# A hybrid encoder block on one core: folds of the long convolutions made two jobs ahead, inverse results handled behind the next job's products, inverse tables loaded with the forward ones

## The chip, the core and the metric

The kernel runs on one core of a Trainium2 chip. Five engines work from queues of their own, each in the order of its program: TensorE (PE) multiplies matrices into the eight banks of PSUM, VectorE (DVE), ScalarE (ACT) and GpSimd (POOL) do elementwise work, SyncE (SP) issues most DMAs. ScalarE and GpSimd issue some DMAs too, from the same queues as their arithmetic. An instruction that waits holds up all that stand behind it on its engine. The metric is the device time of one execution in microseconds, as the median of several.

## What is computed

One layer of an encoder block over 512 tokens of width 1024: a norm, a wide projection, a gated linear recurrence (branch A), a long convolution branch (branch B), a merge, and a mixture of 16 experts. The change touches branch B alone:

```python
hy = dwconv(hy, conv_b_w[l], conv_b_b[l], ...)        # width-3 convolution along the sequence
v, x1, x2 = jnp.split(hy, HYENA_ORDER + 1, axis=-1)   # each (1, 512, 1024)
z = v
for n, gate in enumerate((x1, x2)):
    k = bidir_kernel(filt[:, n, 0], filt[:, n, 1])    # length 1024
    z = gate * fftconv(z, k, filt_bias[l, n])         # irfft(rfft(z) * rfft(k)) + z * bias
y_b = z @ w_b_out[l]
```

So there are two long convolutions in a row (n = 0, 1), each over 1024 channels, and each followed by a gate.

## The kernel before

**Order.** The scheduler is told to keep the order in which the program emits instructions (`tc.manual_schedule()`, L106). A helper, `Defer` (L71 to L93), holds closures back: `df.at(lag, fn, prio)` queues one, `df.tick()` advances a counter and emits all that are due, by time, then by `prio`, then by age. So the place of a step in each engine's queue is set by the tick at which it falls due.

**The long convolutions as matmuls.** Channels are taken in eight blocks of 128; a job (n, j) is two blocks, i = 2j and 2j + 1, of convolution n. There are eight jobs, (0,0) to (0,3) and then (1,0) to (1,3); the text calls them jobs 0 to 7. Each value is split in a high part (rounded to the matmul's format by ScalarE) and a low part (what is left, by VectorE or GpSimd), and each product is three matmuls. The steps of a job:

- *fold* (`fold`, L490): sums and differences of the two halves of `z`, 128 by 512, mirrored; the sum on VectorE, the difference on GpSimd, into a tile `eo`. Two per job.
- *transposes* (`eo_trans`, L496): four per block on TensorE into one PSUM tile, the high part `eoh` by ScalarE, the low part `eol` by VectorE.
- *forward* (`fwd`, L526): 48 matmuls with the tables FC and FS (high and low parts) into four PSUM tiles. Then the products with the filter's spectrum (`K`, loaded from DRAM by `k_load`, L517), per tile: one multiplication on VectorE (`pr`), two additions on GpSimd (`y`), the high part on ScalarE (`yh`), the low part on VectorE (`yl`).
- *inverse* (`inv`, L569): per block 24 matmuls of `yh` and `yl` with the tables IC and IS.
- *result* (`inv_post`, L585): a copy on ScalarE (`qs`), two additions and a multiply-add on VectorE (`yt`), the gate's multiplication on GpSimd (`z`). For n = 0 this `z` is what job (1, j) folds; for n = 1 it is stored to DRAM (`z2d`) by a DMA that ScalarE issues (i < 6) or GpSimd (i = 6, 7).

**The loop** (L761 to L773). Per job: folds of the next job; forward and products of this one; loads of the next K; two projections (`x_slot`, 24 matmuls each, from the list `fill`), which give the gates x1 and x2 of later jobs and whose width-3 convolution (`conv3`: ScalarE, then two multiply-adds on VectorE) falls due one tick later; two inverses. The transposes of the next job fall due at the tick of the first projection (lag 2 in `job_prep`), the result of each inverse one tick after it: the first at the second inverse's tick, the second at the next forward's tick, ahead of the products.

**Weights of the projections** (`ahead`, L247). A projection's weights are loaded by SyncE into a ring (`wring`), split by ScalarE (high) and GpSimd (low) into `whl`, two projections ahead. `ahead` runs in each `slot()` (every projection) and in `fwd_slot`. The next high part waits until the projection that used its buffer has ended.

**Ahead of the loop** (L708 to L717). After the filter stage the tables FC and FS are loaded from GpSimd's queue, the first K from SyncE's, job 0 is folded, and two projections run, with the split of FC and FS between them. IC and IS are loaded from SyncE's queue behind the products of job 0 and split by ScalarE and GpSimd.

**Behind the loop** one projection runs (L931), then the gates of the recurrence (`lru_gates`, L828), whose operands VectorE casts (`wg_prep`, `parts_of`). The expert weights are loaded much later, from L1080 on.

**Buffers.** PSUM has eight banks in one pool (`ps_`, L148); a new tile takes the bank whose last reader stands first in the order of the program.

Of the kernel before, what the change touches and what calls it, by code (L numbers as in the profile page):

```python
# [12 lines left out]
F32R = mybir.dt.float32r  # L13
# [21 lines left out]
for _n, _w in (("g_mix", 8), ("ca_w", 32), ("ca_b", 8), ("b_r", 16), ("b_i", 16), ("lam", 16),  # L35
# [13 lines left out]
    "zz": ("left", dict(z=9, gx=6)),  # L49
# [4 lines left out]
    "H": ("left", dict(eo=2, pr=2, eoh=2, eol=2, FCh=1, FCl=1, FSh=1, FSl=1, K=4, y=2, yh=5, yl=5, ICh=1, ICl=1,  # L54
# [47 lines left out]
def block_kernel(ctx, tc, A, out, dbg=None):  # L102
# [34 lines left out]
    def f(ap):  # L137
        return ap.bitcast(F32)
# [251 lines left out]
    def table_load(nm, q):  # L390
        r = t_([128, 2, 512], nm="pr").rearrange("p a b -> p (a b)")
        q.dma_start(out=r, in_=A[nm])
        return r

    def table(nm, shape, r=None):
        r = table_load(nm, SY) if r is None else r
        r = r.rearrange("p (a b) -> p a b", a=shape[1])
        h = t_(shape, F32R, nm=nm + "h")
        l = t_(shape, F32R, nm=nm + "l")
        act(h, r)  # L400
        tt(G, l, r, f(h), ALU.subtract)
        return h, l
# [106 lines left out]
    def job_prep(n, j):  # L509

        for i in (2 * j, 2 * j + 1):
            eo = fold(zt[n, i])
            df.at(2, lambda i=i, eo=eo: eo_trans(n, i, eo))
# [173 lines left out]
    for q, (n, hf) in enumerate(jobs):  # L687
# [13 lines left out]
        if q < 3:  # L701
            parts = filt_prep(*wfb[q + 1])
            fill.pop(0)() if q < 2 else df.tick()
        else:
            df.tick()
        filt_b(n, hf, 1, im)
# [3 lines left out]
    tabs = [table_load(nm, G) for nm in ("FC", "FS")]  # L710
    k_load(0, 0)
    job_prep(0, 0)
    fill.pop(0)()
    FC = table("FC", [128, 2, 512], tabs[0])
    FS = table("FS", [128, 2, 512], tabs[1])
    fill.pop(0)()
    assert not fill  # L717

    def inv_slot(n, i):
        df.tick()  # L720
        p = inv(n, i)
        df.at(1, lambda: inv_post(n, i, p))

    def fwd_slot(n, j):
        ahead()
        df.tick()
        fwd(n, j)
# [33 lines left out]
    for q, (n, j) in enumerate(cjobs):  # L761
        if q + 1 < 8:
            job_prep(*cjobs[q + 1])
        fwd_slot(n, j)
        if q == 0:
            IC = table("IC", [128, 4, 256])
            IS = table("IS", [128, 4, 256])
        if q + 1 < 8:
            k_load(*cjobs[q + 1])
        for _ in range(2):  # L770
            fill.pop(0)()
        inv_slot(n, 2 * j)
        inv_slot(n, 2 * j + 1)  # L773
# [772 lines left out]
```

## Time and profile before

| | us |
|---|---|
| median of 3 runs | 1643.46 (1640.3 to 1644.1) |
| the profiled execution | 1639.69 |
| its span, from the first to the last instruction | 1637.9 |
| TensorE busy | 1545.1 (94%) |
| VectorE busy | 592.6 (36%) |
| GpSimd busy | 374.0 (23%) |
| ScalarE busy | 371.2 (23%) |
| mean granted clock of TensorE | 0.977 |

The shares are means over stages that differ. Up to about 690 us TensorE has what it needs in SBUF and the DMAs move 85 to 230 GB/s; from there on the expert weights stream in at some 427 GB/s. The long convolutions lie between 136 and 352 us. The profile's views give, for each engine, busy time in a stretch, the single instructions with the idle time ahead of them and what ended it, and the spread of one instruction's length.

### The profile page before, as it was taken

How to read it: one execution, taken by the hardware profiler on the slowest of the kernel's cores; microseconds unless marked ns; L12 is line 12 of the kernel's file. 1: busy time of each engine (PE TensorE's matmuls, PEld its weight loads, DVE VectorE, ACT ScalarE, POOL GpSimd, SP SyncE). 2: the span in 40 equal slices, each digit the busy share in tenths (PEclk: the TensorE clock that was granted, in tenths of full speed). 3: DMA queues.
4: the chain of work that ended last, by engine and by line, in shares of the span. 5: the costliest groups of instructions: out<-in, count | busy, mean ns of one | idle time of the engine just before them, and what ended most of it. 6: DMA issues, size and time to landing. Idle time of an engine off the chain costs nothing.

```text
span 1637.9 us, 17943 instructions
## 1 busy us (share of the span) xinstructions
PE 1545.1 (94%) x7364; PEld 895.4 (55%) x7364; DVE 592.6 (36%) x878; ACT 371.2 (23%) x576; POOL 374.0 (23%) x257
## 2 busy tenths in 40 slices
PE   7999899999999999899999999999999999989997
PEld 5788888888888888733443343343343343333332
DVE  7887778776676644321001101101002002011102
ACT  5543323337655633301010000100100100100011
POOL 3647565655567742000000000000000000000000
PEclk9999999999999999999999999999999999999999
DMA  6566523443433336879999999999999999999996
GB/s 200 155 202 210 154 85 109 142 142 92 114 90 92 90 101 224 351 297 387 407 426 427 426 428 426 428 426 427 427 427 428 426 426 428 427 427 427 426 425 269
DMA packets 140813, 492.26 MB, mean 301 GB/s; under 512 B 8674, under 2 KB 103202, under 8 KB 115644
## 3 DMA queue, kind: packets, MB, share of 16 engines
q1 hardware_dynamic: 138048, 487.34, 75.7%
q0 software_dynamic: 592, 2.07, 0.4%
q10 hardware_dynamic: 2092, 1.72, 0.3%
q8 instruction: 58, 0.95, 0.2%
q14 instruction: 23, 0.19, 0.0%
HBM read 473.82 MB, written 17.30 MB: 300 GB/s over the span
## 4 chain that ended last, share of the span: by engine, by line
PE 49%; DMA 12%; DVE 2%; issue 1%; ACT 1%; POOLq 0%; ACTq 0%; DVEq 0%; SPq 0%
PE q L1261 23%; PE q L1296 11%; DMA we<-in_w_up_dram 6%; PE q L1311 4%; PE ps L244 3%; PE ps L1117 3%; PE q L1227 2%; DMA hz<-in_w_up_dram 2%; DMA whl<-in_w_down_dram 2%; DMA hz<-in_w_down_dram 2%; PE q L1283 1%; PE q L1354 1%; DMA out_dram<-hh 0%; DVE pm L1177 0%; PE q L1246 0%
## 5 line engine op out<-in xcount | busy, mean ns | idle before, releaser
L1261 PE MATMUL q<-we,xe 128*64 128x512 f32 x1088 | 340.6, 597 | 17.8 <-DMA we<-in_w_up_dram 8.1
L244 PE MATMUL ps<-hT,whl 128*128 128x512 f32 x1320 | 307.5, 392 | 0.6 <-POOL whl L132 0.6
L244 PEld LDWEIGHTS ps<-hT,whl 128*128 128x128 f32 x1320 | 248.4, 189 | 53.8 <-POOL whl L132 1.1
L132 POOL TENSOR_TENSOR whl<-wring,whl 128x1024 fp32r<-128x1024 f32 x72 | 181.0, 2517 | 146.2 <-ACT whl L129 66.7
L1465 POOL DMA_INDIRECT out_dram<-we,idx x1 | 1.1, 1097 | 925.5 <-DVE we L135 925.5
L1261 PEld LDWEIGHTS q<-we,xe 128*64 128x64 f32 x1088 | 103.8, 137 | 190.9 <-issue 172.6
L1296 PE MATMUL q<-we,sgy 128*64 128x512 f32 x576 | 183.2, 621 | 4.2 <-ACT sgy L129 3.6
L132 DVE TENSOR_TENSOR xe<-q,cv 128x512 f32<-128x512 f32 (+1 forms) x22 | 11.5, 543 | 468.8 <-PE q L1261 427.0
L1261 PE MATMUL q<-hz,xe 128*64 128x512 f32 x480 | 160.3, 603 | 3.6 <-DMA hz<-in_w_up_dram 2.7
L129 ACT ACTIVATE sgy<-q 128x512 f32<-128x512 f32 x80 | 45.2, 596 | 394.9 <-PE q L1283 221.5
L132 DVE TENSOR_TENSOR xm<-xm,q 128x512 f32<-128x512 f32 x56 | 38.5, 687 | 208.1 <-PE q L1311 208.1
L1261 PE MATMUL q<-wring,xe 128*64 128x512 f32 x240 | 109.4, 604 | 0.8 <-DVE xe L132 0.8
L129 ACT ACTIVATE pm<-q 128x512 f32<-128x512 f32 x7 | 4.2, 597 | 454.4 <-PE q L1246 403.1
L1296 PEld LDWEIGHTS q<-we,sgy 128*64 128x64 f32 x576 | 54.1, 142 | 84.2 <-issue 76.1
L129 ACT ACTIVATE whl<-wring 128x1024 fp32r<-128x1024 f32 x72 | 76.2, 1058 | 91.1 <-PE ps L244 46.8
L1261 PE MATMUL q<-whl,xe 128*64 128x512 f32 x208 | 93.3, 596 | 3.4 <-issue 2.0
L244 PE MATMUL ps<-hA,whl 128*128 128x512 f32 x384 | 89.2, 391 | 0.0
L1261 PEld LDWEIGHTS q<-hz,xe 128*64 128x64 f32 x480 | 48.2, 138 | 62.6 <-issue 55.9
L244 PEld LDWEIGHTS ps<-hA,whl 128*128 128x128 f32 x384 | 72.1, 188 | 15.8
L1296 PE MATMUL q<-hz,sgy 128*64 128x512 f32 x224 | 75.2, 612 | 1.5 <-ACT sgy L129 1.5
L1311 PE MATMUL q<-sgy,pm 128*128 128x512 f32 x112 | 62.7, 642 | 0.0
L1296 PE MATMUL q<-whl,sgy 128*64 128x512 f32 x128 | 61.2, 623 | 1.5 <-DMA whl<-in_w_down_dram 1.5
(316 smaller groups left out, 2071.2 us busy)
## 6 DMA issues: line engine op xcount, KB each, us to landing
we<-in_w_down_dram SPq DMA_DIRECT2D x36, 2048.0 KB, 30.9
we<-in_w_up_dram SPq DMA_DIRECT2D x35, 2048.0 KB, 29.1
we<-in_w_gate_dram SPq DMA_DIRECT2D x33, 2048.0 KB, 29.1
wring<-in_w_in_dram SPq DMA_DIRECT2D x56, 512.0 KB, 4.8
hz<-in_w_gate_dram SPq DMA_DIRECT2D x14, 2048.0 KB, 27.8
hz<-in_w_down_dram SPq DMA_DIRECT2D x12, 2048.0 KB, 31.3
hz<-in_w_up_dram SPq DMA_DIRECT2D x12, 2048.0 KB, 28.3
whl<-in_w_gate_dram SPq DMA_DIRECT2D x8, 2048.0 KB, 30.7
```

The costliest lines, as they stand in the source:

```text
L129: P.activation(out=out, in_=in_, func=func, **kw)
L132: e.tensor_tensor(out=out, in0=a, in1=b, op=op)
L244: T.matmul(p, lhsT=a[:, k, :], rhs=b[k], start=(n == 0), stop=(n == 23))
L1117: T.matmul(p, lhsT=a[k][:, i * 128:(i + 1) * 128], rhs=wo[q][b][:, k, :], start=(n == 0), stop=(n == 23))
L1227: T.matmul(p[:, k * 128:(k + 1) * 128], lhsT=src[:, i, u * 128 * R + r:(u + 1) * 128 * R:R], rhs=pm[:, i, :], start=(i == 0), stop=(i == 3))
L1261: T.matmul(out[q][o:o + 64], lhsT=xe[:, k, o:o + 64], rhs=w[:, r * 2048 + q * 512:r * 2048 + (q + 1) * 512], start=(k == 0), stop=(k == KT ...
L1283: T.transpose(p[:, j * 128:(j + 1) * 128], sg[:, u * 128 * RD + i:(u + 1) * 128 * RD:RD], ident)
L1296: T.matmul(acc[hf][o:o + 64], lhsT=st[:, j % 4 * 128 + o:j % 4 * 128 + o + 64], rhs=w[:, i * 1024 + hf * 512:i * 1024 + (hf + 1) * 512], s ...
L1311: T.matmul(p, lhsT=sc[:, i * 128:(i + 1) * 128], rhs=ye[:, hf * 512:(hf + 1) * 512], start=True, stop=True)
L1354: T.matmul(p, lhsT=pm[:, i, :], rhs=xm[:, i, hf * 512:(hf + 1) * 512], start=(i == 0), stop=(i == 3))
L1465: G.indirect_dma_start(out=out, out_offset=bass.IndirectOffsetOnAxis(ap=last["idx"], axis=0), in_=yo, in_offset=None, bounds_check=S - 1, ...
```

## The change

Four things are moved.

- **Folds.** `job_prep` is split in `job_fold` and `job_turn`. Job q + 2 is folded between the two inverses of job q (job 0 in the filter stage, job 1 between the splits of FC and FS). The transposes of job q + 1 fall due at the tick of job q's second projection, so they come between the two projections and no longer ahead of both. The pool of `eo` is opened earlier for that.
- **Results.** The results of both inverses fall due at the tick of the next job's first projection (lags 3 and 2, with priority 0), behind the next products. For job 7 the lags stay 1.
- **Tables.** IC goes into a tile of its own (`raw`), IS in two halves into the two `xa` tiles, all issued from GpSimd's queue with FC and FS, and their low parts are made by VectorE ahead of job 0.
- **Weights.** `ahead` moves from `fwd_slot` to `inv_slot`.

```diff
@@ -46,12 +46,12 @@
     "W": ("right", dict(wring=1, whl=1)),
     "A": ("right", dict(hT2=1)),
     "bx": ("right", dict(xa=2)),
-    "zz": ("left", dict(z=9, gx=6)),
+    "zz": ("left", dict(z=9, gx=6, eo=2)),
     "S": ("left", dict(Sh=1, Sl=1, S0=1)),
     "F0": ("right", dict(x=4, junk=1, zT=1, w2=1, sa=1, sk=1, s=2)),
     "F": ("left", dict(dec=4, wf=1, wb=1, wc=2, wst=4, ed=4, KCh=1, KCl=1, KSh=1, KSl=1, pr=1, EDh=8, EDl=8, bs=2,
                        kr=3, ki=4)),
-    "H": ("left", dict(eo=2, pr=2, eoh=2, eol=2, FCh=1, FCl=1, FSh=1, FSl=1, K=4, y=2, yh=5, yl=5, ICh=1, ICl=1,
+    "H": ("left", dict(pr=2, raw=1, eoh=2, eol=2, FCh=1, FCl=1, FSh=1, FSl=1, K=4, y=2, yh=5, yl=5, ICh=1, ICl=1,
                        ISh=1, ISl=1, qs=1, yt=2)),
     "mB": ("left", dict(mB=8, hF=8, tg=3)),
     "hA": ("left", dict(hA=8)),
@@ -387,18 +387,18 @@
         return out
 
 
-    def table_load(nm, q):
-        r = t_([128, 2, 512], nm="pr").rearrange("p a b -> p (a b)")
+    def table_load(nm, q, tag="pr"):
+        r = t_([128, 2, 512], nm=tag).rearrange("p a b -> p (a b)")
         q.dma_start(out=r, in_=A[nm])
         return r
 
-    def table(nm, shape, r=None):
+    def table(nm, shape, r=None, e=G):
         r = table_load(nm, SY) if r is None else r
         r = r.rearrange("p (a b) -> p a b", a=shape[1])
         h = t_(shape, F32R, nm=nm + "h")
         l = t_(shape, F32R, nm=nm + "l")
         act(h, r)
-        tt(G, l, r, f(h), ALU.subtract)
+        tt(e, l, r, f(h), ALU.subtract)
         return h, l
 
 
@@ -506,11 +506,15 @@
         act(hi[:, :, c0:c0 + 128], pv)
         tt(V, lo[:, :, c0:c0 + 128], pv, f(hi)[:, :, c0:c0 + 128], ALU.subtract)
 
-    def job_prep(n, j):
-
-        for i in (2 * j, 2 * j + 1):
-            eo = fold(zt[n, i])
-            df.at(2, lambda i=i, eo=eo: eo_trans(n, i, eo))
+    eos = {}
+
+    def job_fold(n, j):
+
+        eos[n, j] = [fold(zt[n, 2 * j + e]) for e in range(2)]
+
+    def job_turn(n, j):
+        for e, eo in enumerate(eos.pop((n, j))):
+            eo_trans(n, 2 * j + e, eo)
 
     Ks, Y = {}, {}
 
@@ -703,26 +707,38 @@
             fill.pop(0)() if q < 2 else df.tick()
         else:
             df.tick()
+            job_fold(0, 0)
         filt_b(n, hf, 1, im)
         df.tick()
     close_("F", "S")
     open_("H", "bx")
     tabs = [table_load(nm, G) for nm in ("FC", "FS")]
+    tabs.append(table_load("IC", G, "raw"))
+    half = [t_([128, 512], nm="xa") for _ in range(2)]
+    for a in range(2):
+        G.dma_start(out=half[a], in_=A["IS"][:, a * 512:(a + 1) * 512])
     k_load(0, 0)
-    job_prep(0, 0)
     fill.pop(0)()
     FC = table("FC", [128, 2, 512], tabs[0])
+    job_turn(0, 0)
     FS = table("FS", [128, 2, 512], tabs[1])
+    job_fold(0, 1)
     fill.pop(0)()
     assert not fill
-
-    def inv_slot(n, i):
+    IC = table("IC", [128, 4, 256], tabs[2], V)
+    IS = [t_([128, 4, 256], F32R, nm=nm) for nm in ("ISh", "ISl")]
+    for a in range(2):
+        h, l = (v[:, 2 * a:2 * a + 2].rearrange("p a b -> p (a b)") for v in IS)
+        act(h, half[a])
+        tt(V, l, half[a], f(h), ALU.subtract)
+
+    def inv_slot(n, i, lag):
+        ahead()
         df.tick()
         p = inv(n, i)
-        df.at(1, lambda: inv_post(n, i, p))
+        df.at(lag, lambda: inv_post(n, i, p), 0)
 
     def fwd_slot(n, j):
-        ahead()
         df.tick()
         fwd(n, j)
 
@@ -759,18 +775,18 @@
         return proj(hTh, hTl)
 
     for q, (n, j) in enumerate(cjobs):
-        if q + 1 < 8:
-            job_prep(*cjobs[q + 1])
         fwd_slot(n, j)
-        if q == 0:
-            IC = table("IC", [128, 4, 256])
-            IS = table("IS", [128, 4, 256])
         if q + 1 < 8:
             k_load(*cjobs[q + 1])
-        for _ in range(2):
-            fill.pop(0)()
-        inv_slot(n, 2 * j)
-        inv_slot(n, 2 * j + 1)
+        fill.pop(0)()
+        if q + 1 < 8:
+            df.at(1, lambda v=cjobs[q + 1]: job_turn(*v))
+        fill.pop(0)()
+
+        inv_slot(n, 2 * j, 3 if q < 7 else 1)
+        if q + 2 < 8:
+            job_fold(*cjobs[q + 2])
+        inv_slot(n, 2 * j + 1, 2 if q < 7 else 1)
 
     for _ in rates:
         pass
```

## Rows read from the trace of the kernel before

**Rows 1.** Windows of four jobs: window, length, busy PE PEld DVE ACT POOL, PEclk, DMA share

```profile
150.21:176.04 25.83, 23.80 (x154) 21.49 (x153) 17.94 (x26) 10.97 (x15) 15.49 (x12) 1.00 0.63 185
...
227.65:254.07 26.42, 24.09 (x155) 21.43 (x153) 21.67 (x34) 7.39 (x12) 15.36 (x14) 1.00 0.34 100
...
305.73:329.04 23.31, 23.31 (x154) 21.39 (x153) 18.74 (x24) 7.50 (x12) 15.00 (x14) 1.00 0.49 139
...
329.04:352.10 23.06, 22.69 (x147) 20.59 (x145) 16.46 (x21) 5.86 (x9) 13.43 (x13) 1.00 0.24 77
```

**Rows 2.** Timeline of PE, 141 to 170 and 305 to 330: start, length, what, idle before

```profile
141.93 0.60 PE L503 MATMUL ps<-ident,eo 128*128 128x128 f32 x4
...
144.28 0.63 PE L503 MATMUL ps<-ident,eo 128*128 128x128 f32 x4 [1.75 <-DVE eo L132]
...
144.66 5.72 PE L244 MATMUL ps<-hT,whl 128*128 128x512 f32 x24
...
311.49 1.03 PE L503 MATMUL ps<-ident,eo 128*128 128x128 f32 x8
...
312.28 11.18 PE L244 MATMUL ps<-hT,whl 128*128 128x512 f32 x48
...
323.29 0.64 PE L578 MATMUL ps<-ICh,yh 128*128 128x256 f32 x4
```

**Rows 3.** Waits, 136 to 350 us: engine, line, awaited, total, times, longest

```profile
PE ps L503 <- POOL eo L132: 5.2, 5, 1.5
...
PE ps L578 <- ACT yh L129: 4.5, 6, 1.0
```

**Rows 4.** Timeline of DVE and ACT, products of jobs 0 and 6

```profile
155.16 2.34 DVE L132 TENSOR_TENSOR pr<-ps,K 128x1024 f32<-128x1024 f32 x2
...
313.12 2.34 DVE L132 TENSOR_TENSOR pr<-ps,K 128x1024 f32<-128x1024 f32 x2
...
321.64 2.10 DVE L132 TENSOR_TENSOR yl<-y,yh 128x512 fp32r<-128x512 f32 x2 [0.86 <-ACT yh L129]
...
322.38 0.63 ACT L129 ACTIVATE yh<-y 128x512 fp32r<-128x512 f32 x1 [0.77 <-POOL y L132]
```

**Rows 5.** Groups by shape, 136 to 352 us: busy, mean ns, idle before

```profile
L135 DVE SCALAR_TENSOR_TENSOR gx<-ps,cv,gx 128x511 f32<-128x511 f32 x30 | 22.3, 747 | 5.4 <-ACT gx L129 4.8
...
L132 DVE TENSOR_TENSOR yt<-ps,qs 128x256 f32<-128x256 f32 x30 | 11.2, 414 | 6.1 <-ACT qs L129 6.1
...
L132 DVE TENSOR_TENSOR eol<-ps,eoh 128x512 fp32r<-128x512 f32 x16 | 10.3, 683 | 5.3 <-ACT eoh L129 5.3
...
L129 ACT ACTIVATE qs<-ps 128x256 f32<-128x256 f32 x15 | 5.8, 385 | 23.3 <-DVE yt L132 21.3 <-issue 1.3 <-PE ps L578 0.5
```

**Rows 6.** Spread of single instructions (ns, min/median/max), by tile, 130 to 360 us

```profile
L132 DVE TENSOR_TENSOR eo<-z x16: 414/1498/2574, 139.5 to 307.5; 128x256 f32<-128x256 f32 x16
...
L135 DVE SCALAR_TENSOR_TENSOR yt<-z,cv,yt x16: 750/754/1935, 180.4 to 353.6; 128x512 f32<-128x512 f32 x16
...
L132 POOL TENSOR_TENSOR z<-yt,gx x16: 1281/1297/1412, 181.2 to 354.4; 128x512 f32<-128x512 f32 x16
...
L132 DVE TENSOR_TENSOR yl<-y,yh x32: 672/966/1276, 158.6 to 346.6; 128x512 fp32r<-128x512 f32 x32
```

**Rows 7.** Timeline of ACT behind the first stored result

```profile
286.29 1.06 ACT L129 ACTIVATE whl<-wring 128x1024 fp32r<-128x1024 f32 x1 [8.79 <-POOL z L132]
```

**Rows 8.** Timeline of POOL around the forward tables' loads

```profile
129.86 0.80 POOL L392 DMA_DIRECT2D pr<-in_FC_dram  x1
...
138.94 2.42 POOL L132 TENSOR_TENSOR whl<-wring,whl 128x1024 fp32r<-128x1024 f32 x1 [6.27 <-ACT whl L129]
```

**Rows 9.** Timeline of DVE and PE at the hand-over behind the loop

```profile
356.26 3.10 DVE L816 CAST xh<-xa 128x512 fp32r<-128x512 f32 x1
...
359.50 0.47 PE L837 MATMUL ps<-xh,wgh 128*128 128x512 f32 x1 [1.77 <-DVE xh L816]
```

**Rows 10.** SyncE's own waits, 130 to 800 us

```profile
SPq L1040 <- DVE hT L132: 16.6, 1, 16.6
```

## The prediction

> **What bounds the kernel now.** I read the page first: by its shares TensorE is the busiest engine by far, so time can be gained only where it stands still, or where what feeds it ends last. The change touches one stage, the eight jobs of the long convolutions. So I next cut that stage into one window per job, from the first forward matmul of a job to that of the next [rows 1]. The reader is to see three things there. The granted clock is 1.00 (the 2.4 GHz level) in all of them, so nothing is lost to the clock. No other engine comes near to being full: VectorE 16.5 to 21.7 us of about 25, GpSimd 13 to 15, ScalarE 6 to 11. And the windows have unlike lengths though the matmuls are the same: job 6 takes 23.31 us with TensorE busy all of it, while jobs 0 to 5 all take longer, job 3 the longest with 26.42.
>
> Job 6 is the yardstick: 5.76 us forward (to the first transpose), 0.79 transposes, 11.01 for two projections, 5.75 for two inverses [rows 2]. Job 7 has no transposes for a next job, so its clean length is 23.31 - 0.79 = 22.52. The waits of TensorE say what the others lose: transposes wait for a fold on GpSimd, inverses wait for the last product's high part on ScalarE [rows 3]. A stall costs more than its listed idle, because the pipeline refills; so I price by window lengths, not by listed waits.
>
> **The change, part by part.**
>
> *Stalls taken away.* From the start of job 0 to the end of job 7 it is 352.10 - 150.21 = 201.89 us; clean it would be 7 x 23.31 + 22.52 = 185.69. Excess: 16.20. Ahead of job 0, the second set of transposes waited 1.75 us for a fold [rows 2]; from 141.93 (where they begin, 0.60 long for the first four) to the next projection it was 144.66 - 141.93 = 2.73 where 0.79 would do: 1.94. Together 18.14 us, if every stall goes and none comes.
>
> *Folds two jobs ahead.* A fold is emitted between the two inverses of job q and used by the transposes of job q+1, some 12 us after the next forward part begins. It stands on VectorE behind the convolution of the second projection, on GpSimd behind a weight's low part; nothing needs it for half a job. The transposes stop waiting.
>
> *Results handled behind the next products.* Where does the wait for the products go? Now VectorE and GpSimd finish the previous job's results before they start the products. In the changed order the first product can start 1.44 us after the forward part begins (12 of the 48 matmuls), say at 1.5. From the start of a product chain to the end of its last high part it is 323.01 - 313.12 = 9.9 us, to the end of its last low part 10.6 [rows 4]. So they are ready at 11.4 and 12.1, and the first inverse starts at 5.76 + 11.01 + 0.79 = 17.56: 5 us of cover. What is late next is the transposed fold of job q+1: it stands on ScalarE and VectorE behind the results (two of them: per result one 0.39 copy, two adds of 0.41, a 0.75 multiply-add), a convolution (two of 0.75) and, on ScalarE, a weight's high part (1.06) [rows 5 to 7]. In jobs 1 to 4 that gives: results done at about 15.5, convolution 18, low parts (two of 0.68) 19 to 21, needed at 23.31 + 0.48. Cover 3 to 5 us; I take 0.3 us for these jobs, bounds 0 and 3.
>
> *The second half, jobs 5 to 7.* There each result also issues a store from ScalarE's queue, which waits for GpSimd's multiply; now that wait holds a weight's high part back by 8.79 us, with TensorE not noticing [rows 7]. Moved, it holds the second result's copy, the weight, the convolution and the transposed fold. Step by step from the forward start of job 5, with VectorE 0.5 late: products done 12.6; first result's multiply-add 14.2; GpSimd multiply 1.30 [rows 6] 15.5; store issued 15.8; second result 17.8, 19.1, 19.5; weight 20.5; convolution 21.3 on ScalarE; transposed high parts 22.5, in time for 23.31; VectorE's convolution 22.8, low parts 24.1, needed at 23.79: 0.3 late. Then VectorE's second convolution (25.8) and the fold of job 7, beside a weight's low part of 2.4 us on GpSimd [rows 8], to about 27.7: the next products start 2.9 late instead of at 24.8. Job 6 repeats this 2.4 us later: low parts at 26.4, so job 7 starts some 2.3 late. Together 2.6 us; bounds 0 and 5.
>
> *The tables.* The inverse tables leave SyncE's queue for GpSimd's, and their low parts leave GpSimd for VectorE: three more DMA issues, 0.80 us each at most, at about 133 us, where GpSimd stood idle for 6.27 [rows 8]. That idle time hides them; without it they would push the forward tables by 2.4, which have about 2 us of cover. On VectorE three subtractions (1024 + 512 + 512 columns: about 2.7 us at the rate of a 0.68 us, 512-column one) stand ahead of job 0's products. VectorE now starts these 155.16 - 150.21 = 5 us after the forward part [rows 4], because the fold of job 1 is in the way; I expect 5 to 7 after, so the last low part lands at 15.6 to 17.6, against 17.56. I take 0.3 us, bounds 0 and 1.5. The row here: GpSimd's and VectorE's instructions do hold one another, a 0.41 us fold on VectorE takes up to 2.57 and a 0.75 multiply-add up to 1.94 [rows 6]. The Trainium skill ("SBUF — State Buffer", Who interferes with whom) says why this speaks against handing the low parts to VectorE: an instruction of VectorE with two SBUF inputs and one of GpSimd that reads SBUF exclude each other for their whole length. The rows agree. By that rule each of the three subtractions would wait out an instruction of GpSimd, and the term would be nearer its bound of 1.5 than 0.3.
>
> *A weight prepared earlier.* The preparation for the second projection (ScalarE high part, GpSimd low part, one SyncE load of 512 KB) moves from the start of the next job to ahead of the inverses. Its order in each queue against the K loads stays; it costs nothing while ScalarE and GpSimd idle during the inverses, which they do.
>
> *The hand-over.* Behind the last inverse TensorE runs one projection and then waits 1.77 us for a cast on VectorE, which took 3.10 beside a weight's low part on GpSimd [rows 9]. In the changed order VectorE reaches that cast about 3.7 us later after the last inverse (job 7's products start 2.2 late, and job 6's results stand behind them), but that weight is prepared earlier, so the cast should not be held: 0.5 us worse, bounds -1.8 (stall gone) and +3.7.
>
> *Does it reach the end?* From about 690 us the DMAs are full with expert weights, but these loads start only when an earlier stage ends: the first waits 16.6 us for that [rows 10]. So an earlier end of the convolutions moves everything behind it.
>
> **Sum.** 18.14 - 0.3 - 2.6 - 0.3 - 0.5 = 14.4 us. The profiled execution took 1639.69 (span 1637.9 and 1.8 around it): 1625.3 against its own time. The median of the three runs, 1643.46, is 3.8 above that execution; taken from the median, 1629.1. With all bounds good it is 18.14 + 1.8 = 19.9 less (1623.5), with all bad 18.14 - 13.2 = 4.9 less (1638.5).
>
> **Rivals.**
>
> *The second half gives most of it back.* If ScalarE's wait for each stored result costs 3 us in each of jobs 5 to 7, not 2.6 in all, 9 us go, and the gain is 8: 1635.5 (1633 to 1638). For it: nine moved instructions stand in one chain there, and the cover that I reckon is under 1 us. Against: job 7 has no transposes to be late with.
>
> *The banks.* Two result tiles now stay in PSUM across the next forward part. If the eight banks were handed out strictly in turn, the second transposes and the second projection would take these two banks and wait for the results: about 1.1 + 1.0 us in four jobs, about 4.2 in two, 17 in all, and nothing is left: 1643. Against it: in the program of before, a new tile takes the bank whose last reader stands first in program order; so handed out, the tiles that wait are others.
>
> *VectorE becomes the bound: slower.* Its work per job is about 21 us, with waits behind GpSimd; the new order removes its slack at the job's end. If most instructions with two SBUF inputs met one of GpSimd (yl 0.68 to 1.28, multiply-adds 0.75 to 1.94, folds 0.41 to 2.57 [rows 6]), a job would be 28 us of VectorE. From (201.89 + 1.94) / 8 = 25.5 us a job on, the change is slower than before; at 26.5 it is 8 us more: 1651. That is also what the skill's rule of the paragraph on the tables would give, were these meetings the common case. Against: in the windows of before such waits are already in the 21 us.
>
> *It doesn't reach the end*, for instance because the weight stream makes up its own time: 1642. Against it stands the wait of [rows 10].
>
> **How the numbers follow.** My forecast (1623 to 1633) gets 0.74, the give-back 0.14, the banks 0.04, not reaching the end 0.04, VectorE as the bound 0.04. Some 0.3%, about 5 us, is what a measurement of this kernel can tell from none. Faster by more: 0.74 + 0.14 = 0.88; within: 0.08; slower: 0.04. The range goes from the good end, 1623, to 1637, which takes in most of the give-back.
>
> **What would show it.** In the profile after: windows of 23.3 to 23.6 us for jobs 0 to 5; no wait of transposes on a fold, and none of inverses on a high part; a new wait of the forward matmuls on VectorE's low part of the transposed fold, 1 to 3 us, at the start of job 7; the last inverse ending at about 338 instead of 352.10, and the first expert load earlier by as much. It is wrong if new waits of TensorE appear in jobs 1 to 4 (transposes or projections waiting for a result's reader would be the banks; inverses waiting for low parts would be VectorE), or if the jobs end 14 us earlier and the end does not.

## The result, and the profile after

The changed kernel takes 1654.22 us (median of 4 runs, 1652.86 to 1658.64); the kernel before, beside it, 1641.88 (4 runs, 1638.94 to 1644.1). The ratio is 1.0091, with a 95% interval of 1.0074 to 1.0107: slower by 0.9%, where a gain of 0.9% was forecast. The profiled execution of after took 1658.64 (span 1656.9). It is the longest of its four, so the two profiled executions lie 18.95 us apart where the medians lie 12.3 apart.

The windows of after: first the stretch from the projection of x(0,1) to job 0, then jobs 0 to 7; columns as in [rows 1].

```profile
139.73:159.07 19.34, 13.72 (x57) 10.95 (x56) 8.34 (x14) 7.37 (x10) 7.06 (x5) 0.85 0.93 316
159.07:190.02 30.95, 25.63 (x154) 23.00 (x152) 28.11 (x34) 9.43 (x14) 19.21 (x17) 0.93 0.48 135
190.02:213.34 23.32, 23.32 (x154) 21.34 (x153) 19.56 (x23) 7.50 (x12) 15.46 (x14) 1.00 0.41 113
213.34:238.02 24.68, 23.58 (x155) 21.40 (x153) 22.18 (x31) 7.38 (x12) 13.93 (x14) 1.00 0.37 101
238.02:266.50 28.48, 25.00 (x155) 22.81 (x153) 25.34 (x37) 7.50 (x12) 16.56 (x16) 0.94 0.35 98
266.50:291.25 24.75, 23.59 (x155) 21.41 (x154) 22.28 (x30) 7.39 (x12) 14.00 (x14) 1.00 0.34 100
291.25:317.41 26.16, 23.74 (x154) 21.36 (x153) 17.81 (x34) 5.94 (x11) 11.36 (x13) 1.00 0.36 108
317.41:342.25 24.84, 23.79 (x152) 21.46 (x152) 16.69 (x23) 7.50 (x13) 15.10 (x15) 1.00 0.43 128
342.25:366.09 23.84, 22.79 (x146) 20.68 (x146) 15.67 (x21) 7.05 (x11) 12.91 (x13) 1.00 0.21 67
```

Job 1 is the clean window that was forecast for all of them (23.32, TensorE busy throughout). Job 0 has grown by 5.1 us against [rows 1], and job 3 takes 28.48 with VectorE "busy" 25.34, at a granted clock of 0.94. What TensorE waits for in after, 136 to 420 us:

```profile
PE ps L541 <- DVE eol L132: 9.7, 6, 3.5
PE ps L244 <- ACT whl L129: 7.5, 2, 5.3
PE ps L244 <- POOL whl L132: 5.6, 1, 5.6
PE ps L853 <- DVE xh L832: 3.3, 1, 3.3
PE ps L541 <- ACT eoh L129: 0.5, 1, 0.5
```

The waits of [rows 3] are gone: no transpose waits for a fold, no inverse for a high part. Others stand in their place: the forward matmuls wait for the low part of the transposed fold (six times), the projections for a weight (whl).

The same stretches of the profiled executions of six kernels, in us; four of these kernels are told of below. The borders are the start of x(0,1)'s projection, the first forward matmul of a job, the end of the last inverse and the end of the span:

| stretch | before | after | rates late in before | that + tables | that + folds and results | last version |
|---|---|---|---|---|---|---|
| x(0,1) to job 0 | 13.74 | 19.34 | 13.82 | 19.69 | 11.79 | 11.79 |
| job 0 | 25.83 | 30.95 | 25.82 | 30.55 | 27.64 | 23.61 |
| jobs 1 to 4 | 103.48 | 101.23 | 97.89 | 95.65 | 93.29 | 93.30 |
| jobs 5 and 6 | 49.52 | 51.00 | 48.25 | 48.24 | 53.32 | 46.66 |
| job 7 | 23.06 | 23.84 | 23.04 | 23.02 | 22.66 | 22.42 |
| last inverse to the end | 1285.80 | 1290.81 | 1285.19 | 1285.11 | 1290.32 | 1287.45 |
| sum | 1501.43 | 1517.17 | 1494.01 | 1502.26 | 1499.02 | 1485.23 |

After stands 15.74 us behind before in the sum: +5.60, +5.12, -2.25, +1.48, +0.78, +5.01. (The profiled execution of after also comes to the first border 3.3 us later. Of the change only the fold of job 0 and the first table loads are issued ahead of that border; in the kernels below that have both, it lies at 134.0 to 137.1 us, beside 136.47 in before and 139.73 in after. So these 3.3 us are no part of the change.) Four places are to be explained.

**Ahead of job 0.** Timeline of GpSimd and TensorE in after:

```profile
152.00 1.07 POOL L719 DMA_DIRECT2D xa<-in_IS_dram  x2 [15.16 <-DVE gx L135]
153.09 2.35 POOL L132 TENSOR_TENSOR whl<-wring,whl 128x1024 fp32r<-128x1024 f32 x1
...
155.49 0.79 PE L244 MATMUL ps<-hT,whl 128*128 128x512 f32 x1 [5.62 <-POOL whl L132]
```

GpSimd stands 15.16 us at the load of the IS halves, and the low part of the next projection's weight stands behind that load. The halves' tiles lie where the filter stage's last result tiles (`ki`) lay, which have to be stored first; the row of an experiment below names these stores.

**In job 0.** Timeline of VectorE, ScalarE and TensorE in after:

```profile
159.34 5.64 DVE L132 TENSOR_TENSOR ISl<-xa,ISh 128x512 fp32r<-128x512 f32 x2 [6.41 <-ACT ISh L129]
...
175.46 0.63 ACT L129 ACTIVATE yh<-y 128x512 fp32r<-128x512 f32 x1 [0.79 <-POOL y L132]
175.99 1.99 ACT L129 ACTIVATE whl<-wring 128x1024 fp32r<-128x1024 f32 x2
...
177.08 1.21 PE L244 MATMUL ps<-hT,whl 128*128 128x512 f32 x2 [5.32 <-ACT whl L129]
```

The weight of job 0's second projection is prepared behind all four high parts of the products, since in the first job nothing prepared it ahead. These products are late themselves: VectorE first makes the low parts of IS, 5.64 us for a pair that takes 1.28 in a kernel below, while GpSimd works without a pause until 163.8. So the first product begins at 166.34, 7.3 us after the forward part.

**Jobs 2 to 5.** Timeline of VectorE, GpSimd and TensorE in after, ahead of job 2, which starts at 213.34:

```profile
206.40 1.29 DVE L631 TENSOR_SCALAR sp<-sp 128x16 f32<-128x16 f32 x1
207.72 2.32 DVE L132 TENSOR_TENSOR sp<-sp,sp 128x16 f32<-128x16 f32 x1
210.08 2.32 DVE L631 TENSOR_SCALAR sp<-sp 128x16 f32<-128x16 f32 x1
...
207.62 4.75 POOL L132 TENSOR_TENSOR whl<-wring,whl 128x1024 fp32r<-128x1024 f32 x2
...
215.09 0.50 PE L541 MATMUL ps<-eol,FCh 128*128 128x256 f32 x2 [1.10 <-DVE eol L132]
```

`sp` are the 16-column tiles of the decay rates, a computation for a later stage that is dealt out in small steps behind each projection. Alone such a step takes 0.17 us; here three take 5.9, and the last two end with GpSimd's two low parts (210.04 and 212.40 against 212.37 for the pair). Behind them VectorE's convolution and the low part `eol` come late for the next job. In job 3 that wait was 3.48 us, and behind it pairs of the same matmuls took 0.63 us up to 245.29 and 0.40 later: the granted clock of that window is 0.94.

**The granted clock.** Three of these stalls cost more than their idle time. Windows of after that begin within or at the end of the waits of 5.62, 5.32 and 3.48 us, columns as in [rows 1]:

```profile
153.20:160.10 6.90, 4.61 (x13) 3.83 (x14) 0.76 (x1) 0.64 (x2) 6.90 (x4) 0.51 1.01 345
177.10:180.50 3.40, 3.40 (x8) 2.73 (x9) 3.33 (x3) 2.52 (x4) 3.39 (x2) 0.50 0.36 102
242.00:245.40 3.40, 3.26 (x15) 3.26 (x16) 3.26 (x10) 0.00 (x0) 0.00 (x0) 0.50 0.00 0
```

TensorE had stood still, and the clock was then at its lower level (1.2 GHz) for 3.4 to 6.9 us. TensorE is busy for 11.27 us in these windows; at the full clock half of that, 5.6 us, would not be there (an estimate from these rows). In the jobs of before the clock was 1.00 throughout [rows 1].

**Behind the loop.** Timeline of ScalarE, SyncE and TensorE in after (last inverse ends at 366.09):

```profile
359.55 0.33 ACTq L601 DMA_DIRECT2D z2d<-z  x1
360.00 0.38 ACT L129 ACTIVATE qs<-ps 128x256 f32<-128x256 f32 x1 [3.75 <-POOL z L132]
363.37 0.33 ACTq L601 DMA_DIRECT2D z2d<-z  x1
...
364.76 0.76 ACT L129 ACTIVATE xa<-ps,cv 128x512 f32<-128x512 f32 x1
...
374.96 4.64 SPq L803 DMA_DIRECT2D hA<-z2d  x8
...
392.83 11.18 PE L244 MATMUL ps<-hT,whl 128*128 128x512 f32 x48 [2.17 <-ACT whl L129]
```

ScalarE stands at the stores of job 6's results until GpSimd's z is made (3.75 us ahead of the second copy), so `xa`, then VectorE's last results, then the gate weights are late; the loads of z, queued behind these weights' load on SyncE, start 8.9 us after the last inverse. In before, whose last inverse ends at 352.10, it was 4.7:

```profile
356.80 3.78 SPq L787 DMA_DIRECT2D hA<-z2d  x8
```

### The profile page after: what moved, and what is told of

Same layout as the page of the kernel before. It is cut to its first block, busy times and chain, and to the rows that moved or that the text cites. A ratio compares the mean times of both kernels' runs of the same rounds, so it can differ in the third digit from the quotient of the medians.

```text
span 1656.9 us, 17972 instructions
## 1 busy us (share of the span) xinstructions
PE 1552.2 (94%) x7364; PEld 901.1 (54%) x7364; DVE 601.2 (36%) x881; ACT 371.3 (22%) x577; POOL 370.5 (22%) x258
## 4 chain that ended last, share of the span: by engine, by line
PE 49%; DMA 12%; DVE 2%; issue 1%; ACT 1%; POOLq 0%; SPq 0%; ACTq 0%; DVEq 0%
PE q L1277 22%; PE q L1312 12%; DMA we<-in_w_up_dram 8%; PE q L1327 4%; PE ps L244 3%; PE ps L1133 3%; DMA hz<-in_w_up_dram 2%; DMA hz<-in_w_down_dram 2%; PE q L1243 2%; PE q L1299 1%; PE q L1370 1%; DMA out_dram<-hh 0%; PE q L1262 0%; DVE pm L1193 0%; DVE m L1190 0%
## 5 line engine op out<-in xcount | busy, mean ns | idle before, releaser
L1277 PE MATMUL q<-we,xe 128*64 128x512 f32 x1088 | 344.4, 607 | 19.2 <-DMA we<-in_w_up_dram 9.5
L244 PEld LDWEIGHTS ps<-hA,whl 128*128 128x128 f32 x384 | 72.1, 188 | 15.8
L132 POOL TENSOR_TENSOR y<-pr 128x256 f32<-128x256 f32 x64 | 50.2, 811 | 48.3 <-DVE pr L132 45.6
```

The source lines that it names most:

```text
L132: e.tensor_tensor(out=out, in0=a, in1=b, op=op)
L244: T.matmul(p, lhsT=a[:, k, :], rhs=b[k], start=(n == 0), stop=(n == 23))
L1277: T.matmul(out[q][o:o + 64], lhsT=xe[:, k, o:o + 64], rhs=w[:, r * 2048 + q * 512:r * 2048 + (q + 1) * 512], start=(k == 0), stop=(k == KT ...
```

## The experiments

Medians in us; the runs of before are those taken beside the kernel. A difference between two changed kernels is given by their medians; by the ratios it comes out up to 2 us otherwise.

| kernel | median (runs) | before (runs) | ratio (95%) |
|---|---|---|---|
| IS halves from SyncE | 1650.70 (4) | 1638.92 (19) | 1.0068 (1.0051 to 1.0085) |
| weight first | 1654.48 (4) | 1638.92 | 1.0083 (1.0063 to 1.0102) |
| rates late | 1642.95 (10) | 1638.92 | 1.0022 (1.0011 to 1.0034) |
| these three | 1635.10 (10) | 1638.92 | 0.9982 (0.9969 to 0.9995) |
| rates late in before | 1631.55 (6) | 1638.70 (13) | 0.9954 (0.994 to 0.9967) |
| three + stores by GpSimd | 1630.87 (6) | 1638.70 | 0.995 (0.9935 to 0.9966) |
| three + later splits | 1633.01 (8) | 1638.70 | 0.9963 (0.9949 to 0.9978) |
| three + both | 1627.30 (6) | 1638.70 | 0.9926 (0.9914 to 0.9939) |
| rates late in before + tables | 1639.74 (11) | 1639.02 (21) | 1.0004 (0.9995 to 1.0013) |
| rates late in before + folds, results | 1636.62 (11) | 1639.02 | 0.9974 (0.9964 to 0.9984) |
| last version: three + later splits + stores by SyncE | 1623.26 (4) | 1639.02 | 0.9894 (0.9879 to 0.9909) |

**Three suspects, one by one, on the changed kernel.** First the IS halves' loads:

```diff
-    for a in range(2):
-        G.dma_start(out=half[a], in_=A["IS"][:, a * 512:(a + 1) * 512])
     k_load(0, 0)
+    for a in range(2):
+        SY.dma_start(out=half[a], in_=A["IS"][:, a * 512:(a + 1) * 512])
```

> The changed kernel with one thing undone in part: the two halves of the table IS are loaded from SyncE's queue, behind the first K loads, instead of from GpSimd's. In the changed kernel GpSimd stands still for 15.16 us ahead of these two loads, since their tiles lie where the last filter results wait to be stored; a weight's low part behind them holds TensorE for 5.62 us. Theory (GpSimd's queue is blocked by the two loads): that stall of TensorE goes, job 0 starts some 6 us earlier, and of that 3 to 7 us reach the end, as the products of job 0 may then be late elsewhere: 1648 to 1651 against 1654. Rival (the three table loads take DMA time from the filter stores, whose landing holds VectorE for 6.42 us instead of 2.80, and all behind it is late): less than 2 us gained, the stall ahead of job 0 replaced by another.

The stretch ahead of job 0 went from 19.34 to 11.78 and GpSimd's wait is gone, so its cause is shown. But job 0 grew from 30.95 to 35.72, now with this wait of the projection:

```profile
PE ps L244 <- ACT whl L129: 11.7, 2, 9.9
```

Of 7.6 us only some 3.8 reach the end (0.0023 of the time by the ratios, not much more than their intervals leave open): the weight of job 0 is late anyway. So second, the weight:

```diff
     for q, (n, j) in enumerate(cjobs):
+        if q == 0:
+            ahead()
         fwd_slot(n, j)
```

> The changed kernel, with the weight of job 0's second projection prepared ahead of job 0's forward part, as in the kernel before, instead of behind its products. In the changed kernel TensorE waits 5.32 us there for the weight's high part on ScalarE. Theory (in the first job the weight has no earlier place, so its preparation stands behind four product high parts on ScalarE): that stall goes, the window of job 0 falls from 31 us to 24 to 27, 4 to 7 us less in all: 1647 to 1650. Rival (job 0 is late anyway, as its products start 7 us after the forward part; the wait moves to the inverses): job 0's window falls by less than 2 us.

Job 0 fell to 24.95, but job 1 rose to 30.67 (in after 30.95 and 23.32): VectorE comes to the low parts `eol` of job 1 at 184.82, in after at 184.49, so its late work had only been put off. The 4 to 7 us that were expected did not come; 1.0083 against 1.0091 is no difference that is clear of the noise. One of the two alone moves the wait on. Third, the small steps:

```diff
         x_slot(n, i)
-        next(rates, None)
-        next(rates, None)
...
             job_fold(*cjobs[q + 2])
+        for _ in range(4):
+            next(rates, None)
```

> The changed kernel, with the small decay-rate steps of VectorE (four sets a job in jobs 0 to 4, 128 by 16) emitted behind the folds instead of behind the two projections. In the changed kernel these small instructions, 0.17 us long, take 1.3 to 2.3 us each, as they stand beside two weights' low parts on GpSimd, and the low parts of the transposed fold behind them come 1.1 to 3.5 us late for the forward matmuls of jobs 2 to 4. Theory (the small steps are what makes the transposed fold late): no wait of the forward matmuls on VectorE in jobs 1 to 4, windows of 23.3 to 24 us there instead of 23.3 to 28.5, some 6 to 9 us less: 1645 to 1648. Rival (the results moved behind the products are themselves what makes it late): the waits stay at 1 us or more and less than 3 us is gained.

11.3 us (0.0069), the largest of the three and more than expected: jobs 1 to 4 take 23.32, 23.33, 23.33 and 23.33. The wait for `eol` has gone from 9.7 to what jobs 6 and 7 have:

```profile
PE ps L541 <- DVE eol L132: 2.1, 2, 1.1
```

All three together:

> The three edits together: halves of IS from SyncE's queue, job 0's second weight ahead of its forward part, small decay-rate steps behind the folds. If the three causes are what turned the forecast gain into a loss, 15 to 20 us go: 1634 to 1639, faster than the kernel before by 3 to 8 us; what is left is the second half, where ScalarE waits for each stored result (waits of 1 us for the transposed fold in jobs 6 and 7), and the hand-over. If they overlap or each uncovers the next wait, under 10 us go and the kernel stays slower than the one before.

1635.10, 0.2% faster than before, and the approach to job 0 is 11.80. Left over: job 0 with 28.36, jobs 5 and 6 with 25.08 and 26.14, and the stretch behind the last inverse with 1290.2.

**Are the small steps a cost of the change?** The same move in the kernel before:

```diff
         x_slot(n, i)
-        next(rates, None)
-        next(rates, None)
...
         inv_slot(n, 2 * j)
+        for _ in range(4):
+            next(rates, None)
         inv_slot(n, 2 * j + 1)
```

> The kernel before, with only the four small decay-rate steps of a job moved: from behind each projection's slot to between the job's two inverse slots. Theory: in the kernel before these steps are held by GpSimd just as much (20 us of VectorE in all, single ones 2.3 us) but they stand where VectorE has idle time of 4.4 us, so moving them changes the time by less than 1 us; it is the deferral of the results that puts work of the bound chain behind them. Rival: the steps cost the kernel before several us too, and the 11 us that the same move gave in the changed kernel are nothing of the change: then this kernel is 4 to 11 us faster than before, with jobs 1 to 4 at 24 to 25 us instead of 25.4 to 26.4.

The theory fell, and the rival's 4 to 11 us came: the kernel before loses 7.15 us to them too. Timeline of VectorE and GpSimd in the kernel before, in job 2:

```profile
224.15 2.39 DVE L627 TENSOR_SCALAR sp<-sp 128x16 f32<-128x16 f32 x1
...
224.11 2.40 POOL L132 TENSOR_TENSOR whl<-wring,whl 128x1024 fp32r<-128x1024 f32 x1 [2.66 <-ACT whl L129]
```

This held convolution, results and fold, and so the transposes. With the steps moved, TensorE's waits in the kernel before become:

```profile
PE ps L578 <- ACT yh L129: 4.2, 6, 1.0
...
PE ps L503 <- POOL eo L132: 0.3, 1, 0.3
```

against 5.2 us in five waits for the fold [rows 3]. Jobs 1 to 5 shorten from 129.69 to 122.83 us. So the fold was late because of these steps, not because of the order of folds and results. Of the 11.3 us that the move gave in the changed kernel, about 4 are of the change. It had put more behind the steps, and it had made them longer: all steps together take 37.9 us of VectorE in after, 20.8 in before and 9.2 in before with the steps moved. In after GpSimd's two low parts of a job stand in a row beside them (4.75 us for the pair, above); in before they are 11 us apart (198.68 and 209.57).

**The parts alone, on that base (1631.55).** The tables' part (loads on GpSimd's queue and splits ahead of job 0, as in the change):

```diff
     tabs = [table_load(nm, G) for nm in ("FC", "FS")]
+    tabs.append(table_load("IC", G, "raw"))
+    half = [t_([128, 512], nm="xa") for _ in range(2)]
+    for a in range(2):
+        G.dma_start(out=half[a], in_=A["IS"][:, a * 512:(a + 1) * 512])
...
     assert not fill
+    IC = table("IC", [128, 4, 256], tabs[2], V)
...
         fwd_slot(n, j)
-        if q == 0:
-            IC = table("IC", [128, 4, 256])
-            IS = table("IS", [128, 4, 256])
```

> The kernel before with the decay-rate steps late, and of the change the tables' part alone, as the change has it: IC and the IS halves loaded from GpSimd's queue with the forward tables, split on ScalarE and VectorE ahead of job 0. Base is the kernel before with the rate steps late (1631.55). Theory: by the changed kernel's own trace, GpSimd stands at the load of the IS halves until the filter stage's stores have landed, and the next weight's low part behind it; the stretch from x(0,1)'s projection to job 0 grows by 3 to 6 us (13.8 in the base, 19.3 in the changed kernel), job 0 gains at most 2.1 (the inverses' waits for ICl 1.4 and ISl 0.7), so this kernel is 1 to 4 us slower than its base, 1632.5 to 1636. Rival: the tables' part is worth what the forecast put on it, a gain of 1 to 2 us, about 1630, and what the changed kernel loses ahead of job 0 comes of the weight's moved preparation.

8.2 us slower than its base, more than twice what was expected. By the table 5.87 us are lost ahead of job 0 and 4.73 in it. GpSimd's wait is there, and named by the stores that end it. GpSimd's fold for job 0's second block stands behind that load; VectorE's fold of job 1 stands behind the split of IC:

```profile
POOL xa L714 <- DMA kd<-ki: 15.0, 1, 15.0
...
PE ps L503 <- POOL eo L132: 6.3, 1, 6.3
PE ps L503 <- DVE eo L132: 4.6, 1, 4.6
...
152.10 10.52 DVE L132 TENSOR_TENSOR ICl<-raw,ICh 128x1024 fp32r<-128x1024 f32 x1
...
159.16 2.38 POOL L132 TENSOR_TENSOR whl<-wring,whl 128x1024 fp32r<-128x1024 f32 x1
```

That split took 10.52 us; in after it took 1.21, while GpSimd stood at its load. Here GpSimd works off what had piled up behind the load, without a pause from 146.97 to 161.54, and the split ends 1.08 us after that. So the blocked load costs twice: once on GpSimd's own queue, and once on VectorE when the queue is released. Why the split did not get in between two of GpSimd's instructions, as the small steps above did, is not shown.

Jobs 1 and 2 are some 1 us shorter each than in the base, without their waits for `yh`; why is open.

Then the folds and the deferred results, without tables and with the weight's preparation where it was:

```diff
-        for _ in range(2):
-            fill.pop(0)()
-        inv_slot(n, 2 * j)
+        fill.pop(0)()
+        if q + 1 < 8:
+            df.at(1, lambda v=cjobs[q + 1]: job_turn(*v))
+        fill.pop(0)()
+        inv_slot(n, 2 * j, 3 if q < 7 else 1)
+        if q + 2 < 8:
+            job_fold(*cjobs[q + 2])
...
-        inv_slot(n, 2 * j + 1)
+        inv_slot(n, 2 * j + 1, 2 if q < 7 else 1)
```

> The kernel before with the decay-rate steps late, and of the change the folds made two jobs ahead and the results deferred, without the tables' part and with the next weight prepared where the kernel before prepares it. Base is the kernel before with the rate steps late (1631.55). Theory: jobs 1 to 4 go from 24.40, 24.16, 25.16 and 24.17 to 23.3 to 23.4 (4.5 us less), the transposes of job 0's second channel wait 1.8 us less, jobs 5 and 6 go from 24.94 and 23.31 to about 25 and 26 (ScalarE stands at the stores), and the stretch from the last inverse to the end grows by 4 to 5 us, since the last results, and behind them the loads of z, come later after the last inverse: the sum is a gain of about 6 against a loss of 6 to 7, so 1630.5 to 1634. Rival, the forecast's: the hand-over costs 0.5 and the kernel gains 5 us or more, 1626.5 or below.

5.1 us slower than its base (3.3 by the ratios), and above the theory's 1630.5 to 1634. By the table it is -2.03 ahead of job 0 and -4.60 in jobs 1 to 4, as the theory has it, but +1.82 in job 0, +5.07 in jobs 5 and 6, -0.38 in job 7, and +5.13 behind the loop. The forecast's hand-over of 0.5 fell. The waits:

```profile
PE ps L846 <- DVE xh L825: 5.0, 1, 5.0
PE ps L541 <- ACT eoh L129: 2.6, 1, 2.6
```

On this base the two parts lose 8.2 and 5.1 us. The whole change with the rates late stands 11.4 us above the same base (1642.95 against 1631.55), so it loses also where the small steps play no part.

**Taking the last two costs away.** From the version with the three repairs: the stores of the results off ScalarE's queue; the inverse tables' splits behind job 0's forward part; both.

```diff
-            (P if i < 6 else G).dma_start(out=z2d[i], in_=z)
+            G.dma_start(out=z2d[i], in_=z)
```

> The kernel with the three repairs, and the stores of the finished results to z2d all issued from GpSimd's queue, behind the product that makes them, instead of from ScalarE's for the first six. Theory (second half): in the kernel with the three repairs jobs 5 and 6 last 25.08 and 26.14 us against 23.33 for a clean one, because ScalarE stands at each store until GpSimd's z is made (whl 3.41 and qs 3.75 us of idle time in job 7, eoh late by 1.59 in job 6); without it both last 23.3 to 23.9, the end of the last inverse comes 3.5 to 4.5 us earlier, and the time is about 1631 (0.995 of before). Rival: GpSimd pays 0.72 us for each store and is itself late for the y tiles, so jobs 5 and 6 stay at 25 to 26 and the time at 1635; or the hand-over takes it: the inverses end earlier, the gates of the next stage begin when they did, 1635 too.

Jobs 5 and 6: 23.32 and 23.33, the time 4.2 us less (1635.10 to 1630.87), as the theory said, though the stretch behind the loop is now 1292.3. The splits:

```diff
     assert not fill
-    IC = table("IC", [128, 4, 256], tabs[2], V)
...
         fwd_slot(n, j)
+        if q == 0:
+            IC = table("IC", [128, 4, 256], tabs[2], V)
...
```

The lines that split IS move with it.

> The kernel with the three repairs, and the splits of the two inverse tables (ICh, ICl, ISh, ISl) moved on their engines from ahead of job 0's forward products to behind them; their loads stay early. Theory: job 0 lasts 28.36 us against 23.33 because VectorE comes to its first product only at 156.83, 11.0 us after the forward transform began, held by ICl (3.38) and by the wait for the IS data (2.21 and the ISl pair 1.40); with the splits behind, the first product starts about 148.5, the inverses no longer wait for yh (1.89 and 1.04 there), job 0 lasts 23.5 to 25, and the time is about 1631 to 1632. Rival: the inverse tables then come late instead, as in the kernel before (waits of inverses for ICl 1.3 and ISl 0.7), job 0 stays above 26 and the time within 1 us of 1635.

Job 0: 23.49 instead of 28.36; but jobs 5 and 6 took 26.37 and 26.62 here (25.08 and 26.14) and the stretch behind the loop 1292.4 (1290.2), so a part is paid there. The time is 2.1 us less by the medians and 3.1 by the ratios, where 3 to 4 were expected. Both edits:

> Both of the last two edits on the kernel with the three repairs. If the two gains are independent: job 0 near 24 us, jobs 1 to 6 at 23.3 to 23.9, the time near 1627 to 1628, a ratio of 0.993 to before. If either gain is only paid elsewhere (the tables late, the hand-over), it stays at 1631 or above.

1627.30: job 0 takes 24.01, jobs 1 to 6 23.32 to 23.33. Only the stretch behind the loop is still long, 1291.72, since the loads of z on SyncE now wait for stores that land late from GpSimd's queue:

```profile
SPq L806 <- DMA z2d<-z: 3.1, 1, 3.1
```

So last, the first six stores from SyncE:

```diff
+            (SY if i < 6 else G).dma_start(out=z2d[i], in_=z)
```

> The kernel with the three repairs and the later table splits, and the first six stores to z2d issued from SP's queue in place of ScalarE's (the last two stay on GpSimd's, as they were). Beside the version with all eight on GpSimd's queue (1627.3; from the last inverse to the end 1291.7 us, where the kernel before has 1285.8). Theory: jobs 5 and 6 are clean as there (23.3), and since the loads of z no longer wait for a store that lands late in GpSimd's queue (SP waited 3.1 us there), the stretch after the last inverse is 2 to 4 us shorter: 1623 to 1625.5. Rival: the stretch is set by VectorE's last results and the split of the gate weights, not by that wait: it stays at 1291 and the time at 1627; or SP, standing at a store, is late with the K loads or the weights, and jobs 5 to 7 lengthen.

1623.26, as expected, and 1.1% faster than before: that wait is 1.2 us, and the stretch behind the loop, at 1287.45, is 4.3 us shorter, so the wait is not all of it. Windows of jobs 0, 1 and 6 of this version:

```profile
148.56:172.17 23.61, 23.57 (x154) 21.39 (x153) 19.00 (x23) 10.45 (x15) 18.10 (x15) 1.00 0.85 259
172.17:195.49 23.32, 23.32 (x154) 21.34 (x153) 20.59 (x39) 7.39 (x12) 13.89 (x15) 1.00 0.37 105
...
288.80:312.13 23.33, 23.33 (x155) 21.36 (x154) 20.22 (x24) 7.39 (x12) 17.27 (x16) 1.00 0.55 160
```

TensorE is busy from end to end, and VectorE at 19 to 21 us a job is not the bound. Two us against the base's 1285.2 behind the loop are left, with one wait of 3.40 for a weight on ScalarE; they were not taken apart.

## Why the prediction was wrong

The forecast's own sum, with each term as the two profiled executions have it: 18.14 - 7.99 (jobs 1 to 4: 101.23 against 4 x 23.31) - 5.70 (jobs 5 to 7: 74.84 against 69.14) - 7.54 (ahead of job 0: 19.34 against 11.80) - 7.64 (job 0: 30.95 against 23.31) - 5.01 (behind the loop) = -15.74, where 14.4 was forecast.

- **The tables, and the weight: 0.3 and nothing were forecast, 15.2 came.** This is the step that failed first. "That idle time hides them" asked only where GpSimd is idle, not what the new loads wait for: their tiles reuse memory of the filter stage, so the queue stands until those stores land. For VectorE's three subtractions "about 2.7 us" were reckoned; they took 1.21 and 5.64 in after, and the first of them 10.52 with the tables alone, beside the work that the load had held back on GpSimd. "It costs nothing" for the weight was reckoned in the steady state; in the first job the preparation had been the first thing of that job and was now behind its products. The part with the tables alone costs 8.2 us. With the rates late these two stretches stand 15.8 us above clean ones (18.86 + 32.09 against 11.80 + 23.31); undoing loads and weight gives 10.8 of that back (to 11.80 + 28.36), the later splits 4.9 more (28.36 to 23.49). What the weight costs by itself is not shown. The filter stage's stores of `kr` also land later, 6.8 us after issue instead of 3.1, but so they do (5.7) with folds and results alone, whose stretch ahead of job 0 is clean.
- **Jobs 1 to 4: 0.3 was forecast (bounds 0 and 3), 7.99 came.** The chain "results done at about 15.5, convolution 18, low parts 19 to 21" left out the small rate steps between results and convolution. They were in the trace of before, with single ones at 2.3 to 2.4 us, but under other lines than the ones listed. The moved weight made them worse: "ScalarE and GpSimd idle during the inverses" is true of these two engines, but VectorE runs the steps there and stood beside GpSimd's two low parts. (That is read from the traces; the weight's place alone was not changed in these jobs.) With the steps out of the way the chain is as reckoned: in the kernel with the rates late four windows of 23.32 to 23.33.
- **Stalls taken away: the size was right, the cause of a good part was not.** Of the 16.20 us in the jobs, 6.86 are owed to the same small steps; the change did not remove these, it put other work behind them. That the rest can go is shown by the last version, whose eight jobs take 185.99 us where 185.69 was called clean. A wait named as "transposes <- fold on GpSimd" says who came last, not why.
- **The second half: 2.6 forecast (bounds 0 and 5), 5.70 came**, with a share of the rate steps in job 5; without those it is 3.41 (48.72 + 23.83 against 69.14). The mechanism was the forecast's, shown by the stores moved: the term was mis-sized.
- **The hand-over: 0.5 (bounds -1.8 and 3.7), 5.01 came.** It looked at the cast on VectorE alone. The results that come later also hold the gate weights, behind these on SyncE the loads of z, and behind those on ScalarE the next weights. With the stores off ScalarE's queue and on SyncE's some 3 us of it go; 2.3 against the base stay.
- **The clock: nothing was forecast.** "Nothing is lost to the clock" was read from before, where it holds. The new stalls brought the lower level with them, for an estimated 5.6 us, which are contained in the terms above.
- **What held.** The waits for folds and high parts vanished; no wait for a bank came, so that rival fell; a new wait for `eol` of 1 to 3 us at job 7 was foretold and is there (but in six jobs); what happens in the loop reaches the end, less or more only by the hand-over (last line but one of the table).

The rival that came nearest is "VectorE becomes the bound: slower" (1651). Its lock is real, but its place was another: not the many middle-sized instructions of each job but steps of 0.17 us, and the tables' splits ahead of job 0's products. The Trainium skill ("SBUF — State Buffer", Who interferes with whom) counts `tensor_scalar` and `cast` among the instructions of VectorE that can exclude GpSimd's, beside those with two SBUF inputs; the rows agree, a `tensor_scalar` of 16 columns took 2.39 us, as long as GpSimd's instruction beside it. The prediction let each of the three subtractions wait out one instruction of GpSimd; the rows show one of them held by a whole row of such instructions, 10.52 us.

## What to carry to other kernels

An instruction that is issued earlier must be followed through everything it waits for, its destination's memory included, and everything that is queued behind it; idle time of the queue hides nothing if the instruction itself has to wait. Steady-state reckoning leaves out the first and the last turn of a loop, where this change lost 15 and 5 us. And before a wait is credited to the change, ask what made the awaited step late: here moving four sets of tiny steps in each job gave the old kernel 7 us without any of the change.

## What the runs showed of the hardware

- Steps of 0.17 us on VectorE (128 x 16) took up to 2.4 us beside a GpSimd subtraction of 1024 columns: 17 scalar steps at lines 631 and 644 of after took 14.4 us, and in the kernel with the rates late 3.0.
- A subtraction of 1024 columns on VectorE, both inputs in SBUF, took 1.21 us while GpSimd stood, 3.38 beside one such instruction of GpSimd and 10.52 beside a row of them without a pause; in the last two cases it ended 1.1 us after GpSimd's last.
- Behind stalls of TensorE of 5.62, 5.32 and 3.48 us the granted clock was 0.50 for 6.9, 3.4 and 3.4 us.
- A load in GpSimd's queue that waits for its tile stops the arithmetic behind it as well, for 15 us here; a store in ScalarE's queue did the same for 3.75 us.
- Which queue issues six stores of 256 KB moved this kernel by about 10 us (1633.01 from ScalarE, 1623.26 from SyncE). SyncE stood at these six for 32.7 us in all, and jobs 1 to 6 stayed at 23.32 to 23.33.
